# Two weight sums of a row formed before the next row's, operand steps taken two a row up to the fifth warm-up row, and operand sums held behind output weights

## The chip, the cores and the metric

The kernel runs on one core of one Trainium2 chip. The metric is the device time of one execution in microseconds (us). Three runs of the kernel before gave 2141.2, 2142.65 and 2145.68 us; the median is 2142.65 us. A run of this kernel can tell a difference of about 0.2% (4.3 us) from no change.

## The reference, cut to what matters

One Conformer-style layer over 1152 token columns (1024 of a prompt and 8 x 16 of running streams), all in fp32: a SwiGLU half step, a mixer (a gated delta rule beside pooling), a second SwiGLU half step, a final norm.

```python
def swiglu(x, w_gate, w_up, w_down):
    return (jax.nn.silu(x @ w_gate) * (x @ w_up)) @ w_down
...
x = x + 0.5 * swiglu(rms_norm(x, norm_ffn1[l]), w_ffn1_gate[l], w_ffn1_up[l], w_ffn1_down[l])
m, s_new, conv_new, pool_new = mixer(rms_norm(x, norm_mix[l]), ...)
x = x + m
x = x + 0.5 * swiglu(rms_norm(x, norm_ffn2[l]), w_ffn2_gate[l], w_ffn2_up[l], w_ffn2_down[l])
```

The width is 1024 and the hidden width of SwiGLU is 2816, which is 22 rows of 128. All three edits of the change lie in the two half steps; the mixer between them is not touched.

## The kernel before, in words

**Operands in two parts.** TensorE multiplies fp32r values. Each fp32 weight or activation is therefore split in two: ScalarE casts it to a high part (`hi`, line 288 or 186), and VectorE subtracts that from the original to get the low part (`lo`, line 289 or 187). A product is three matmuls: high by high, high by low, low by high (line 59).

**Columns.** The 1152 columns are three chunks: chunk 0 has 512, chunks 1 and 2 have 320 each. Chunks 1 and 2 form the two column halves of a Strassen-Winograd 2 x 2 scheme, in which seven products (named B11, B21, B22, T1, T2, T3, T4) do the work of eight. The code calls this pair "1"; chunk 0, cut in two halves of 256, is pair "0".

**`gate_up`, the first part of a half step.** It forms `silu(x @ w_gate) * (x @ w_up)` row by row.

- Warm-up: the first ten rows are computed for chunk 0 directly, two products of 24 matmuls for each of gate and up. Beside them a generator `build` (the function `operands`) prepares the Winograd operands of pair 1 in 15 steps: norms of chunks 1 and 2 (sums of squares, a 128x1 matmul with `ones`, `rt` on VectorE at line 232, a power on GpSimd at line 233, a matmul with `ident` that spreads it), scaling (line 337), seven combinations (lines 300 to 317) with their splits (line 328). After its end the same calls take up to eight scaling steps (line 372) of `build0`, which prepares the same for pair 0. Lines 605 to 606 call `built()` two or three times a row.
- Row phase: then every row is done in Winograd form, for pair 1 alone (rows 8, 9, 0 to 3), for both pairs (10 to 21), and for pair 1 alone again (4 to 7). In the six rows before the first one with both pairs the remaining 22 steps of `build0` run as well, at four places of a row.

**One row in the row phase (class `Row`).** A row has four weight blocks of 128x512 floats: `w[0]`, `w[1]` from the gate matrix, `w[2]`, `w[3]` from the up matrix. Three blocks go to TensorE as they are (B11, B21, T4) and four as sums, formed by GpSimd:

- sum 1 = `w[2] + w[3]`, for T1 (line 283),
- sum 2 = sum 1 + `w[0]`, for T2 (line 287; one buffer, `sum`),
- sum 4 = sum 2 + `w[1]`, for B22 (line 283),
- sum 3 = `w[0] + w[2]`, for T3 (line 283).

Sums 1, 3 and 4 take the two buffers of the ring `s` (in the region Q) in turn, in the order in which the code asks for them. A sum's buffer is free again when ScalarE and VectorE have split the sum that stood in it. TensorE's order in a steady row is T1 of the next row, T3 of this one, then B11 and B21 of the next, T4 of this one, T2 and B22 of the next. The split operands rotate through seven buffers O0 to O6, so the splits of a row run up to seven products ahead of the matmuls; in the steady rows O0 holds T2, O1 holds B22, O2 holds T1, O3 holds T3, O4 B11, O5 B21 and O6 T4.

**Reading the products.** Four of the products pile up in one PSUM tile: B11, then T2, T3 and T4 are added onto it. Between them VectorE must have read the tile: line 498 (`c2 = al - c3`) after T2 and before T3, line 512 (`c3 = c3 - al`) after T3 and before T4, line 523 after T4. These instructions stand in VectorE's queue among the splits (line 289), the operand steps of `build0` (lines 351, 358, 367) and, for finished groups of two rows, the sums of the generator `combine` (lines 300 to 317, 414, 415). An engine executes its queue in order.

**`downs`, the second part of a half step.** `down0` multiplies chunk 0 by the output weights, whose units are split by `split_unit` (lines 186, 187). Beside it a generator `sums()` takes four groups of raw rows that `gate_up` has put into DRAM (regions x10, x11, x20, x21 after loading, line 846) through `combine` and splits each result (lines 858, 859) into the regions B0 to B6, for `down12` to use later. `tc.issue_after(ins)` is an order for the scheduler: of the instructions in its block, those on the engine of `ins` are put behind `ins`.

Of the kernel before, what the change touches and what calls it, by code (L numbers as in the profile page):

```python
# [7 lines left out]
F32 = mybir.dt.float32  # L8
# [32 lines left out]
def trunk(ctx: ExitStack, tc: tile.TileContext, xin, s0, convst, poolst, cm_in, vec_in, small_in,  # L41
# [3 lines left out]
    V, A, G, T, SY = nc.vector, nc.scalar, nc.gpsimd, nc.tensor, nc.sync  # L45

    class Products:

        t = 0.0
# [98 lines left out]
    W = {}  # L148
# [33 lines left out]
    def split_unit(unit, e=None):  # L182
        i, raw = unit
        m = raw.shape[-1]
        hi, lo = [region(t, F32R)[:, :m] for t in W["splits"][i % len(W["splits"])]]
        A.copy(hi, raw)  # L186
        (e or V).tensor_sub(lo, raw, hi.bitcast(F32))  # L187
        return [t.rearrange("p (k c) -> p k c", c=P) for t in (hi, lo)]

    def load_mix(src, kind):  # L190
# [78 lines left out]
    class Blocks:  # L269


        def __init__(self, ring):
            self.gs, self.ring, self.n, self.e = Slots(), ring, 0, G

        def piece(self, *src, more=None):

            m = src[0].shape[-1]
            t = region(self.ring[self.n % len(self.ring)], F32R)
            self.n += 1
            hi, lo = t[:, :m], t[:, 512:512 + m]  # L280
            if len(src) == 2:
                t = self.gs.get("s", m)
                self.e.tensor_add(t, *src)  # L283
                src = [t]
            src = src[0]
            if more:
                G.tensor_add(more[0], src, more[1])
            Blocks.high = A.copy(hi, src).ins  # L288
            Blocks.mark = V.tensor_sub(lo, src, hi.bitcast(F32)).ins  # L289
            return [x.rearrange("p (k c) -> p k c", c=P) for x in (hi, lo)]  # L290
# [95 lines left out]
    def gate_up(wi, wg, wu, gk, H, RB, cs, ahead, norm, x0=None):  # L386


        bl = Blocks([f"O{(i + 6) % 7}" for i in range(7)])
        gs, piece, product = bl.gs, bl.piece, bl.product  # L390
# [62 lines left out]
        class Row:  # L453
# [19 lines left out]
            def left_gate(self):  # L473

                self.al, self.p1, self.row = {}, {}, {}
                w = piece(self.w[0])
                for c in self.pairs:
                    self.al[c] = self.into("da"[c], c, w, "B11")
                    if c:
                        self.p1[c] = gs.get("p1", N)  # L480
                    else:
                        self.row = cs.get("row", N0)
                        self.p1[c] = self.row[:, :N0 // 2]
                    A.copy(self.p1[c], self.al[c])
                w = piece(self.w[1])
                for c in self.pairs:
                    ga, p1 = self.into("b", c, w, "B21"), self.p1[c]
                    V.tensor_add(p1, p1, ga)
                    A.activation(p1, p1, AF.Silu)

            def right_gate(self):

                self.c2 = {}
                w = piece(self.sm)
                for c in self.pairs:
                    self.c2[c] = gs.get("c2", N) if c else self.row[:, N0 // 2:]
                    product(self.al[c], w, (op0, op)[c]["T2"], False)
                    V.tensor_sub(self.c2[c], self.al[c], self.c3[c])  # L498
                step()
                w = piece(self.sm, self.w[1])  # L500
                for c in self.pairs:
                    de, c2 = self.into("b", c, w, "B22"), self.c2[c]
                    V.tensor_add(c2, c2, de)
                    A.activation(c2, c2, AF.Silu)

            def right_up(self):

                w = piece(self.w[0], self.w[2])
                for c in self.pairs:
                    c2, c3 = self.c2[c], self.c3[c]  # L510
                    product(self.al[c], w, (op0, op)[c]["T3"], False)
                    V.tensor_sub(c3, c3, self.al[c])
                    V.tensor_mul(c2, c2, c3)
                    if c:
                        gated(self.f, 2, c2)
# [77 lines left out]
        for f in range(2 if x0 else 0, ahead):  # L593
            g1, g2, u1, u2 = load(f)
            pg, pu = pt("b")[:, :N0], pt("a")[:, :N0]
            done = gated0(f, pg, pu)
            product(pg, piece(g1), H0[0], True, False)
            product(pg, piece(g2), H0[1], False, True)
            next(done)
            product(pu, piece(u1), H0[0], True, False)  # L600
            built()
            product(pu, piece(u2), H0[1], False, True)
            next(done)
            built()
            if f > 1:
                built()
        for _ in build:
            pass
# [230 lines left out]
    def downs(wd, gk, src, done0=None, after0=lambda: (), done12=None, ends=lambda: None):  # L839
# [12 lines left out]
        def sums():  # L852
            for _ in range(4):
                yield
            for q in range(RAW // 2):
                def put(name, src):
                    hi, lo = [op0[name][s][q] for s in range(2)]
                    A.copy(hi, src)
                    V.tensor_sub(lo, src, hi.bitcast(F32))  # L859

                yield from combine(*stage[q], put)

# [700 lines left out]
    for n in names:  # L1563
        if n[1] in "dHXr":
            continue
        b, w, h = n[0], n[1], n[2]
# [40 lines left out]
    while left or fill or live or cur:  # L1607
# [8 lines left out]
        if cand and (not cand[0][0] or cur is None or cur[1] > cand[0][1]):  # L1616
            n = cand[0][-1]
            e = live[n]
# [204 lines left out]
```

## Time and profile before

| what | value |
|---|---|
| median of three runs | 2142.65 us (2141.2 to 2145.68) |
| the profiled execution | 2141.4 us |
| its span, first to last instruction | 2139.6 us |
| TensorE (PE) busy | 98% of the span |
| VectorE (DVE) busy | 71% |
| ScalarE (ACT) busy | 45% |
| GpSimd (POOL) busy | 23% |
| granted TensorE clock, mean | 0.998 |

The profile calls the engines PE (matmul), PEld (weight load), DVE, ACT, POOL and SP (the queue of the transfers). In a list of waits a row names the engine, the tile that the waiting instruction writes, its line, the engine and line waited for, then the total in us, the count and the longest. In a timeline a row gives the start, the length, the engine, line, operation and tiles, the count of merged instructions and, in brackets, the idle time before and what ended it. In a table of windows each row gives the length of the window and then PE, PEld, DVE, ACT and POOL busy in it.

### The profile page before, as it was taken

Reading aid. Unit: us, or ns where it says so; the run is one execution under the profiler, and the core shown is the slowest. Engines: PE = TensorE matmul, PEld = TensorE weight load, DVE = VectorE, ACT = ScalarE, POOL = GpSimd, SP = SyncE. Lnnn points to the kernel's source line nnn. Section 1 sums busy time; section 2 is a strip of 40 time slices with the busy share of each in tenths; the row PEclk is TensorE's granted clock in tenths of the full one; section 3 lists DMA queues with packets and bytes.
Section 4 is the critical chain, followed back from the end, with each engine's and each line's share of the span. In section 5 each row is a group of like instructions: output and inputs, shape, how many; then the busy total and the mean of one; then the engine's idle time right before and its main releaser. Section 6 shows DMA issues by size and latency. Waiting matters only on the chain.

```text
span 2139.6 us, 34979 instructions
## 1 busy us (share of the span) xinstructions
PE 2100.1 (98%) x13219; PEld 1941.3 (91%) x13219; DVE 1509.4 (71%) x2948; ACT 955.9 (45%) x1974; POOL 496.7 (23%) x471
## 2 busy tenths in 40 slices
PE   9999999999999999999999999999999999999997
PEld 7799999999789998888999998889999999988997
DVE  7989555567537887878687877888955556744887
ACT  6445344444313445645555545544534444422333
POOL 1244343332001200100111100224534333200121
PEclk9999999999999999999999999999999999999999
DMA  7333333357465732112222122443333335746572
GB/s 258 131 114 125 110 119 110 133 197 259 123 239 175 278 99 72 50 61 64 69 91 82 54 92 92 167 138 108 125 110 119 110 134 190 263 131 243 187 275 80
DMA packets 106136, 298.21 MB, mean 139 GB/s; under 512 B 16624, under 2 KB 24688, under 8 KB 105712
## 3 DMA queue, kind: packets, MB, share of 16 engines
q1 hardware_dynamic: 104672, 294.63, 40.1%
q8 instruction: 104, 1.70, 0.3%
q10 hardware_dynamic: 1296, 1.36, 0.2%
q14 instruction: 64, 0.52, 0.1%
HBM read 223.28 MB, written 72.66 MB: 138 GB/s over the span
## 4 chain that ended last, share of the span: by engine, by line
PE 83%; DVE 10%; issue 3%; ACT 2%; POOL 1%; DMA 1%; POOLq 0%; DVEq 0%; SPq 0%; ACTq 0%
PE ps_a L59 32%; PE ps_d L59 21%; PE ps_b L59 19%; PE ps_c L59 10%; DVE O L289 3%; DVE O L187 1%; PE ps_b L63 1%; ACT O L186 0%; DVE A L367 0%; DVE B L1090 0%; DVE A L1229 0%; DVE A L1230 0%; DMA g_keep<-x 0%; ACT O L288 0%; DVE B L859 0%
## 5 line engine op out<-in xcount | busy, mean ns | idle before, releaser
L59 PE MATMUL ps_a<-B,O 128*128 128x320 f32 x3040 | 505.5, 310 | 7.8 <-DVE x L498 5.8
L59 PEld LDWEIGHTS ps_a<-B,O 128*128 128x128 f32 x3040 | 457.1, 188 | 13.2 <-DVE x L498 7.5
L59 PE MATMUL ps_a<-A,O 128*128 128x320 f32 (+1 forms) x2048 | 447.4, 355 | 2.0 <-DVE x L739 1.8
L59 PEld LDWEIGHTS ps_a<-A,O 128*128 128x128 f32 x2048 | 347.1, 189 | 40.1 <-ACT O L288 2.3
L59 PE MATMUL ps_d<-A,O 128*128 128x512 f32 (+1 forms) x1632 | 321.1, 353 | 2.6 <-ACT O L186 1.6
L59 PEld LDWEIGHTS ps_d<-A,O 128*128 128x128 f32 x1632 | 270.5, 189 | 49.0 <-ACT O L186 3.9
L289 DVE TENSOR_TENSOR O<-Q,O 128x512 fp32r<-128x512 f32 (+1 forms) x238 | 197.2, 831 | 109.8 <-ACT O L288 108.9
L288 ACT CAST O<-Q 128x512 fp32r<-128x512 f32 (+1 forms) x238 | 142.8, 604 | 175.6 <-POOL Q L283 43.5
L59 PE MATMUL ps_b<-A,O 128*128 128x256 f32 (+2 forms) x1128 | 208.1, 334 | 5.4 <-ACT O L288 5.3
L289 DVE TENSOR_TENSOR O<-R,O 128x512 fp32r<-128x512 f32 (+1 forms) x204 | 159.9, 789 | 59.0 <-ACT O L288 58.4
L59 PE MATMUL ps_b<-B,O 128*128 128x320 f32 x1248 | 200.8, 309 | 0.0
L59 PEld LDWEIGHTS ps_b<-A,O 128*128 128x128 f32 x1128 | 175.2, 191 | 26.2 <-ACT O L288 5.7
L59 PEld LDWEIGHTS ps_b<-B,O 128*128 128x128 f32 x1248 | 186.4, 188 | 0.0
L288 ACT CAST O<-R 128x512 fp32r<-128x512 f32 (+1 forms) x204 | 123.8, 612 | 105.5 <-PE ps_d L59 34.4
L186 ACT CAST O<-R 128x1024 fp32r<-128x1024 f32 (+1 forms) x86 | 85.8, 1009 | 165.9 <-PE ps_d L59 121.7
L59 PE MATMUL ps_c<-B,O 128*128 128x320 f32 x912 | 144.9, 309 | 0.6 <-DVE O L289 0.6
L59 PEld LDWEIGHTS ps_c<-B,O 128*128 128x128 f32 x912 | 136.0, 188 | 1.3 <-DVE O L289 0.9
L187 DVE TENSOR_TENSOR O<-R,O 128x1024 fp32r<-128x1024 f32 (+1 forms) x86 | 101.8, 1190 | 49.2 <-ACT O L186 29.4
L444 POOL TENSOR_TENSOR A<-A,A 128x512 fp32r<-128x512 f32 x44 | 71.0, 1613 | 248.6 <-ACT A L443 248.4
L59 PE MATMUL ps_d<-B,O 128*128 128x320 f32 (+1 forms) x576 | 117.4, 348 | 0.8 <-DVE x L1111 0.7
L59 PEld LDWEIGHTS ps_d<-B,O 128*128 128x128 f32 x576 | 92.7, 190 | 9.6 <-DVE x L1111 2.1
L414 ACT CAST x<-x 128x320 fp32r<-128x320 f32 x98 | 44.8, 458 | 96.6 <-DVE x L523 32.8
(334 smaller groups left out, 3012.5 us busy)
## 6 DMA issues: line engine op xcount, KB each, us to landing
g_keep<-x SPq DMA_DIRECT2D x98, 320.0 KB, 2.6
R<-in_wu SPq DMA_DIRECT2D x51, 512.0 KB, 3.8
R<-in_wg SPq DMA_DIRECT2D x50, 512.0 KB, 3.8
R<-in_wd SPq DMA_DIRECT2D x48, 512.0 KB, 3.8
g_keep<-A SPq DMA_DIRECT2D x44, 512.0 KB, 3.8
A<-g_keep SPq DMA_DIRECT2D x44, 512.0 KB, 6.0
B<-g_keep SPq DMA_DIRECT2D x56, 320.0 KB, 6.6
A<-g_keep SPq DMA_DIRECT2D x42, 320.0 KB, 4.9
```

What stands on the lines that cost most here:

```text
L59: self.put(nc.tensor.matmul(out, lhs, rhs, **k), n / 2400 + .003 if lhs.dtype == F32R else max(n, lhs.shape[-1]) / 600)
L63: self.put(nc.tensor.transpose(out, lhs, rhs), out.shape[-1] / 1200)
L186: A.copy(hi, raw)
L187: (e or V).tensor_sub(lo, raw, hi.bitcast(F32))
L288: Blocks.high = A.copy(hi, src).ins
L289: Blocks.mark = V.tensor_sub(lo, src, hi.bitcast(F32)).ins
L414: A.copy(go[:, 0], src)
L444: G.tensor_sub(go[:, 1], row, go[:, 0].bitcast(F32))
```

## The change

It has three parts.

1. A method `total` forms a sum of two blocks without splitting it. Sum 4 is now asked for in `left_gate`, right after the split of `w[1]`, and sum 3 in `right_gate`, right after the split of sum 4 and so before the next row's sum 1 and sum 2. The order in which the ring `s` is used becomes sum 4, sum 3, next sum 1, where it was sum 4, next sum 1, sum 3.
2. In the warm-up, the third call of `built()` in a row starts with row 5 instead of row 2 (`f > 4` for `f > 1`). In the first half step the calls of the warm-up are then 22 instead of 25, and one of the eight scaling steps of `build0` moves into the row phase; in the second half step they are 25 instead of 28, and all eight stay.
3. `split_unit` notes its VectorE instruction in `W["mark"]`, and the splits of `sums()` in `down0` are traced under `tc.issue_after(W["mark"])`.

```diff
@@ split_unit
-        (e or V).tensor_sub(lo, raw, hi.bitcast(F32))
+        W["mark"] = (e or V).tensor_sub(lo, raw, hi.bitcast(F32)).ins
@@ class Blocks
+        def total(self, a, b):
+
+            t = self.gs.get("s", a.shape[-1])
+            self.e.tensor_add(t, a, b)
+            return t
+
         def piece(self, *src, more=None):
...
-            if len(src) == 2:
-                t = self.gs.get("s", m)
-                self.e.tensor_add(t, *src)
-                src = [t]
-            src = src[0]
+            src = self.total(*src) if len(src) == 2 else src[0]
@@ Row.left_gate
                 w = piece(self.w[1])
+                self.s4 = bl.total(self.sm, self.w[1])
@@ Row.right_gate
                 step()
-                w = piece(self.sm, self.w[1])
+                w = piece(self.s4)
+                self.s3 = bl.total(self.w[0], self.w[2])
@@ Row.right_up
-                w = piece(self.w[0], self.w[2])
+                w = piece(self.s3)
@@ gate_up, warm-up
             built()
-            if f > 1:
+            if f > 4:
                 built()
@@ downs, sums()
                     hi, lo = [op0[name][s][q] for s in range(2)]
-                    A.copy(hi, src)
-                    V.tensor_sub(lo, src, hi.bitcast(F32))
+                    with tc.issue_after(W["mark"]):
+                        A.copy(hi, src)
+                        V.tensor_sub(lo, src, hi.bitcast(F32))
```

**GpSimd in the row phase.** Before, at row 0 (the third of the row phase). Q is the region of the ring `s`, x21 holds sum 2, R0 to R3 are raw weights.

```order
L287 TENSOR_TENSOR x21_131_996<-Q_46_117,R3_50_121 128x512
L283 TENSOR_TENSOR Q_46_117<-R1_48_119,R2_49_120 128x512
L283 TENSOR_TENSOR Q_46_117<-x21_131_996,R3_50_121 128x512
L283 TENSOR_TENSOR Q_46_117<-R1_48_119 128x512
L287 TENSOR_TENSOR x21_131_996<-Q_46_117,R0_47_118 128x512
```

These are sum 2 of row 0, sum 3 of the row ahead of it, sum 4 of row 0, sums 1 and 2 of the next row. Now, in the same row:

```order
L278 TENSOR_TENSOR Q_46_117<-Q_46_117 128x512
L289 TENSOR_TENSOR x21_131_995<-Q_46_117,R3_50_121 128x512
L278 TENSOR_TENSOR Q_46_117<-R3_50_121,Q_46_117 128x512
L278 TENSOR_TENSOR Q_46_117<-x21_131_995,R3_50_121 128x512
L417 TENSOR_TENSOR x20_130_994<-x10_128_992,x20_130_994 128x320
L278 TENSOR_TENSOR Q_46_117<-R1_48_119 128x512
```

These are sums 1, 2, 3 and 4 of row 0 one after the other (line 278 is the sum, line 289 sum 2), then an operand sum and sum 1 of the next row. A row's four sums now stand together, and sum 1 takes the buffer of the sum 4 ahead of it, where it took that of a sum 3.

**VectorE in the same row.** Its queue has the same kinds of instructions in the same order; only the operand step between two splits is a neighbouring one. Now:

```order
L291 TENSOR_TENSOR O1_151_1202<-Q_46_117,O1_151_1202 128x512
L369 TENSOR_TENSOR A0_153_1221<-x00_33_104,A0_153_1221 128x512
L291 TENSOR_TENSOR O2_154_1226<-Q_46_117,O2_154_1226 128x512
L516 TENSOR_TENSOR x21_131_995<-x21_131_995,ps_a_135_1020 128x320
L517 TENSOR_TENSOR x11_129_993<-x11_129_993,x21_131_995 128x320
L291 TENSOR_TENSOR O3_156_1245<-Q_46_117,O3_156_1245 128x512
```

Before, the same six stood as O1 at line 289, line 367, O2, lines 512 and 513, O3. Between the split of sum 4 (O1) and that of sum 1 (O2) there is one operand step, before and now.

**TensorE in the warm-up.** Before, the 128x1 matmuls of the second norm and the matmuls that spread its result (first half step):

```order
L59 MATMUL ps_d_82_514<-ones_67,B6_66_321 128x1 x3
L59 MATMUL ps_b_85_532<-A0_35_106,O1_87_534 128x512
L59 MATMUL ps_b_85_532<-A2_37_108,O1_87_534 128x512
L59 MATMUL ps_b_85_532<-A0_35_106,O1_87_534 128x512 x2
L59 MATMUL ps_b_85_532<-A2_37_108,O1_87_534 128x512
L59 MATMUL ps_b_85_532<-A0_35_106,O1_87_534 128x512 x2
L59 MATMUL ps_b_85_532<-A2_37_108,O1_87_534 128x512
L59 MATMUL ps_b_85_532<-A0_35_106,O1_87_534 128x512
L59 MATMUL ps_d_84_521<-ident_66,rt_83_518 128x128 x3
```

Now:

```order
L59 MATMUL ps_d_87_565<-ones_67,B6_66_321 128x1 x3
L59 MATMUL ps_a_83_517<-A1_36_107,O4_89_572 128x512
L59 MATMUL ps_a_83_517<-A3_38_109,O4_89_572 128x512
L59 MATMUL ps_a_83_517<-A1_36_107,O4_89_572 128x512 x2
L59 MATMUL ps_a_83_517<-A3_38_109,O4_89_572 128x512
L59 MATMUL ps_a_83_517<-A1_36_107,O4_89_572 128x512 x2
L59 MATMUL ps_a_83_517<-A3_38_109,O4_89_572 128x512
L59 MATMUL ps_a_83_517<-A1_36_107,O4_89_572 128x512 x2
L59 MATMUL ps_a_83_517<-A3_38_109,O4_89_572 128x512
L59 MATMUL ps_a_83_517<-A1_36_107,O4_89_572 128x512
L59 MATMUL ps_d_90_592<-ident_66,rt_88_569 128x128 x3
```

The `ones` group stands 36 matmuls later than before and the `ident` group 39 later; 12 weight matmuls lie between them where 9 did. In the second half step 31 row matmuls are added ahead of the spreading ones.

**ScalarE at the start of `down0`.** Before, ahead of the fourth unit of output weights (O4 from R0), the casts of raw rows from x11 and x10:

```order
L858 CAST B4_449_5236<-x11_442_5226 128x320
L858 CAST B0_445_5232<-x11_442_5226 128x320
L858 CAST B1_446_5233<-x10_441_5224 128x320
L858 CAST B2_447_5234<-x10_441_5224 128x320
L858 CAST B4_449_5236<-x10_441_5224 128x320
L186 CAST O4_463_5310<-R0_454_5243 128x768
```

Now:

```order
L863 CAST B2_447_5234<-x11_442_5226 128x320
L863 CAST B4_449_5236<-x11_442_5226 128x320
L863 CAST B1_446_5233<-x10_441_5224 128x320
L863 CAST B2_447_5234<-x10_441_5224 128x320
L863 CAST B4_449_5236<-x10_441_5224 128x320
L186 CAST O4_463_5310<-R0_454_5243 128x768
```

The three casts from x10 still stand ahead of that unit on ScalarE. On VectorE, whose instruction is the mark, the 28 splits of a half step and the combinations between them are now spread over the units up to the end of `down0`'s first part; before, all but one of them stood ahead of the eighth unit.

## The prediction

> **What bounds the kernel now.** The page comes first: span and busy time by engine.
>
> ```profile
> span 2139.6 us, 34979 instructions
> PE 2100.1 (98%) x13219; PEld 1941.3 (91%) x13219; DVE 1509.4 (71%) x2948; ACT 955.9 (45%) x1974; POOL 496.7 (23%) x471
> ```
>
> PE is the bound. The change neither adds nor removes a matmul, so it can only change how long PE waits, 39.5 us of the span by this line, or runs stretched behind a late operand. The list of PE's waits (total, count, longest) shows which of them the edits can touch.
>
> ```profile
> PE ps_a L59 <- DVE x L498: 5.8, 5, 1.8
> PE ps_b L59 <- ACT O L288: 5.3, 1, 5.3
> PE ps_d L59 <- POOL rt L233: 3.4, 4, 2.4
> PE ps_d L59 <- ACT O L186: 1.6, 3, 1.2
> PE ps_a L59 <- DVE x L512: 1.1, 2, 0.6
> ```
>
> L498 and L512, VectorE's readings of the piled-up products, belong to the row phase (edit 1); rt L233 to the warm-up (edit 2); O L186 to `down0` (edit 3). The 5.3 us of O L288 is one wait. None of the edits moves the kernel's opening, so I leave it. Next the table of windows: the length, then PE, PEld, DVE, ACT and POOL busy, then the granted clock. The first two windows are the six rows for pair 1 alone ahead of the rows with both pairs, in each half step; the third lies in the rows for pair 1 alone at the end; the other four are single steady rows from L498 to L498.
>
> ```profile
> 126.36:205.05 78.69, 75.21 (x506) 73.60 (x505) 78.27 (x103) 41.69 (x84) 39.36 (x28) 1.00 0.38 126
> 1462.85:1540.51 77.66, 73.74 (x493) 72.13 (x492) 76.54 (x103) 41.13 (x83) 39.58 (x28) 1.00 0.37 123
> 470.00:520.00 50.00, 50.00 (x347) 50.00 (x347) 39.44 (x60) 25.33 (x49) 19.45 (x15) 1.00 0.74 261
> 134.70:147.50 12.80, 12.80 (x90) 12.80 (x89) 12.77 (x18) 6.21 (x13) 5.85 (x4) 1.00 0.26 84
> 147.50:163.20 15.70, 14.67 (x97) 13.95 (x96) 15.66 (x23) 7.10 (x15) 8.26 (x6) 1.00 0.38 131
> 163.20:177.80 14.60, 12.82 (x84) 12.32 (x84) 14.57 (x20) 8.94 (x18) 8.56 (x6) 1.00 0.51 179
> 177.80:190.59 12.79, 12.26 (x83) 12.20 (x84) 12.76 (x19) 5.77 (x12) 5.87 (x4) 1.00 0.34 109
> ```
>
> A row of pair 1 has seven products of twelve weight loads, 84, and PEld is busy 12.32 us with them when it is fed. In the six rows DVE is busy 99% (78.27 of 78.69), and PE loses 78.69 − 73.60 = 5.09 us there, in the second half step 77.66 − 72.13 = 5.53, together 10.62. So here DVE sets the pace: the single rows last 12.8 to 15.7 us with DVE full. In the closing rows PE fills its 50.00 us and DVE 39.44: an edit that costs DVE something is paid for in the six rows and hidden there.
>
> **Edit 1: the order of the sums.** Here is DVE's timeline in the first of those single rows (start, length, line, tiles), then POOL's, and one cast of ACT.
>
> ```profile
> 136.10 1.66 DVE L289 TENSOR_TENSOR O<-Q,O 128x512 fp32r<-128x512 f32 x1
> 137.68 0.68 DVE L367 TENSOR_TENSOR A<-x,A 128x512 fp32r<-128x512 f32 x1
> 138.28 1.78 DVE L289 TENSOR_TENSOR O<-Q,O 128x512 fp32r<-128x512 f32 x1
> 139.99 0.47 DVE L512 TENSOR_TENSOR x<-x,ps_a 128x320 f32<-128x320 f32 x1
> 140.50 1.37 DVE L513 TENSOR_TENSOR x<-x,x 128x320 f32<-128x320 f32 x1
> 143.99 1.38 DVE L289 TENSOR_TENSOR O<-R,O 128x512 fp32r<-128x512 f32 x1
> ```
>
> ```profile
> 135.91 1.30 POOL L287 TENSOR_TENSOR x<-Q,R 128x512 f32<-128x512 f32 x1 [4.49 <-issue]
> 137.84 1.68 POOL L283 TENSOR_TENSOR Q<-R,R 128x512 f32<-128x512 f32 x1 [0.63 <-DVE O L289]
> 140.21 1.31 POOL L283 TENSOR_TENSOR Q<-x,R 128x512 f32<-128x512 f32 x1 [0.69 <-DVE O L289]
> 143.25 1.57 POOL L283 TENSOR_TENSOR Q<-R 128x512 f32<-128x512 f32 x1 [1.74 <-DMA R<-in_wu]
> ```
>
> ```profile
> 139.55 0.62 ACT L288 CAST O<-Q 128x512 fp32r<-128x512 f32 x1 [1.49 <-POOL Q L283]
> ```
>
> A DVE instruction of this size with two inputs in SBUF takes 0.68 us free and 1.37 to 1.78 while a POOL sum runs; L512, with one input in PSUM, takes 0.47. L513, half as large, I put at 0.47 free. So the four sums cost DVE 1.66 − 0.68 = 0.98 (sum 2), 1.78 − 0.68 = 1.10 (sum 3), 1.37 − 0.47 = 0.90 (sum 4) and 1.38 − 0.68 = 0.70 (sum 1): 3.68 us a row.
>
> Now with the new order of the ring's two buffers. Sum 1 takes the buffer of the previous sum 4, so it waits until O1 (B22) has been split; before, it waited for a split done long ago, and its result lay ready when DVE came to O2. In DVE's queue O1 and O2 are one operand step apart. From the end of O1: the operand step, 0.60 start to start (137.68 to 138.28); sum 1, 1.30 (the length of 135.91); the cast, 0.62, beside which POOL runs sum 2 at once, 1.30, and blocks the split; the split itself, 0.60. That is 0.60 + 1.30 + 1.30 + 0.60 = 3.80 us from the end of O1 to that of O2. Before it was 2.30 (137.76 to 140.06), and without sums 1.20. Queued behind the waiting split are L512 and all later splits of the row; PE's T3 waits for L498, and T4 for L512. Sums 1 and 2 then cost 2.60, sum 3, now let go by O2, costs L513's 0.90 in sum 4's place, and sum 4, let go by O3, the 1.10 of a split: 4.60. That is 0.92 us a row more than 3.68.
>
> Where DVE is full this is PE's time. Of the six rows, four have the four sums alone: 4 × 0.92 = 3.7. The other two (147.50 and 163.20, POOL x6) have operand sums of `combine` as well, which already spread the sums apart; I take 0.4 for both together. That is 4.1 a half step, **+8.2** in both. Bounds: 0 where the sums cost what they did, and 1.5 (3.80 − 2.30, with nothing saved on sums 3 and 4) in five rows of two half steps, 15.0. I take 8.2, nearer to the middle, because it is the walk along the quoted rows. A gain is the first rival. Where DVE has slack (the closing rows, 39.44 of 50.00) the step costs nothing: PE's operands lie up to seven products ahead. Sums 3 and 4 need no block that the sums 1 and 2 or a split of the row hadn't needed by then, so none of SP's loads is waited for sooner; a load that starts sooner finds the transfer engines 0.26 to 0.51 busy in these rows.
>
> One statement of the Trainium skill speaks on this price: "Perfetto Trace Analysis", section "GPSIMD Engine Instruction", calls recorded spans of that engine unreliable in part. If a sum holds DVE only for the mean 0.92 that DVE loses (3.68 / 4) instead of 1.30, sums 1 and 2 cost 1.84 against 0.98 + 0.70 = 1.68; with sums 3 and 4 at 2.00 the row is 3.84, 0.16 more, and the same rows give 1.4 in place of 8.2.
>
> **Edit 2: the warm-up.** PE's timeline around the second norm of the first half step, the two instructions between, and the same place in the second half step:
>
> ```profile
> 57.07 0.72 PE L59 MATMUL ps_d<-ones,B 128*128 128x1 f32 x6
> 57.65 2.31 PE L59 MATMUL ps_b<-A,O 128*128 128x512 f32 x9
> 62.31 0.93 PE L59 MATMUL ps_d<-ident,rt 128*128 128x128 f32 x6 [2.35 <-POOL rt L233]
> 60.76 0.14 DVE L232 TENSOR_SCALAR rt<-ps_d 128x3 f32<-128x3 f32 x1
> 60.97 1.29 POOL L233 TENSOR_TENSOR rt<-rt,vec 128x3 f32<-128x3 f32 x1 [10.03 <-DVE rt L232]
> 1387.04 0.94 PE L59 MATMUL ps_d<-ident,rt 128*128 128x128 f32 x6 [0.39 <-POOL rt L233]
> ```
>
> DVE's L232 runs at 60.76, 3 us after the `ones` group, because it is queued behind earlier steps; then POOL takes 1.29. Only nine matmuls (2.31 us) cover this. Now twelve do (2.31 × 12 / 9 = 3.08), a row's spacing later when DVE has had fewer steps to run; L232, 0.14, and POOL, 1.29, then fit into 3.08 with 1.65 to spare. So **−2.35** (if DVE were again 3 us late, 3.08 − 3.0 − 1.43 leaves 1.35 of it). In the second half step 31 matmuls more, about 8 us, stand ahead of the spreading ones: **−0.39**. In the first half step one scaling step moves into the DVE-full rows:
>
> ```profile
> L372 DVE SCALAR_TENSOR_TENSOR x<-x,vec,A x8: 740/743/1784, 85.2 to 106.7; 128x512 f32<-128x512 f32 x8
> ```
>
> Its median is 0.74 us; between 0 and that I take **+0.4**, since the last step only slides to the end of the six rows.
>
> **Edit 3: the held splits.** The timeline at the start of `down0`:
>
> ```profile
> 529.99 4.64 DMA x<-g_keep
> 534.62 1.17 ACT B L858 x3
> 535.79 1.68 ACT O L186 x2
> 536.58 1.20 PE L59 MATMUL ps_d<-A,O 128*128 128x512 f32 x4 [1.21 <-ACT O L186]
> ```
>
> The 1.21 us stall comes from ACT: its three casts of raw rows wait for a transfer that ends at 534.62, and the unit's cast L186 stands behind them. The mark is an instruction of DVE, so only DVE's halves of the splits are held; in ACT's order the three casts stand ahead of L186 as before. So the stall stays: **0**, between −0.4 (less DVE work between the units) and +0.6 (a split of the next units later). In the second half step this stage loses a few tenths at most. The held DVE work must be done before `down12` and has the rest of `down0` as cover.
>
> **The sum.** The profiled execution took 2141.4 us, 1.8 more than its span. 2141.4 + 8.2 + 0.4 − 2.35 − 0.39 + 0 = 2147.3. The median of the runs shown is 2142.65, 1.25 above: **2148.5 us**.
>
> **The rivals.**
>
> *Faster: forming the sums ahead takes POOL's chain off ACT and DVE.* The page's group of casts waits for those sums most:
>
> ```profile
> L288 ACT CAST O<-Q 128x512 fp32r<-128x512 f32 (+1 forms) x238 | 142.8, 604 | 175.6 <-POOL Q L283 43.5
> ```
>
> If the early sums 3 and 4 let DVE run ahead, PE's 10.62 us shrink; all of it with edit 2 gives 2142.65 − 2.74 − 10.62 = 2129.3, half 2134.6. Against it: PE's waits name DVE's L498 and L512, not POOL or ACT O in this stage, and DVE is 99% busy, so ready operands don't help it. It decides if DVE's loss a row falls from 3.68 below 3.68 − (12.80 − 12.32) = 3.2, where the shortest of these rows comes down to PE's 12.32. Chance 0.2.
>
> *The same: each sum costs DVE what it did.* The blocked time only changes its place; edit 2 remains: 2142.65 − 2.74 = 2139.9. For it: four sums a row, before and after. Against it: before, each sum cost 0.70 to 1.10 of its 1.3, partly hidden beside L512 and idle moments, and the new chain leaves none for sums 1 and 2. Chance 0.32. The Trainium skill, "SBUF — State Buffer", section "Who interferes with whom", says that a DVE instruction with two SBUF inputs and a GpSimd one that reads SBUF exclude each other for a whole instruction, and one with a single SBUF input isn't touched. By that rule each sum costs up to its whole length wherever it stands, which is this rival; the trace agrees on which are blocked (1.37 to 1.78 against L512's 0.47).
>
> *Slower* is the forecast, 0.48. Its mechanism shows from (4.3 + 2.74 − 0.4 − 0.8) / 8 = 0.73 us more a row on: below that, the gain of edit 2 and the 4.3 us that can be told from no change cover it.
>
> **How the numbers follow.** The forecast's own range is the sum with 0 to 15.0 for edit 1: 2140.3 to 2155.3. The whole range reaches down to half of the faster rival, about 2135, and up to 2155. About 0.2% (4.3 us) is what a measurement can tell from no change; that band is 2138.4 to 2146.9. Faster needs the first rival at nearly half strength: 0.2. The same takes the second rival's 0.32 and 0.03 of the forecast, where its price is small: 0.35. Slower: the other 0.45.
>
> **What would show it.** In the changed profile: six-row windows longer by some 4 us each with PEld unchanged; 3.8 us between the ends of O1's and O2's splits; O2's cast waiting for POOL and sum 1 for DVE's O1; PE's wait at the second norm gone; the stall after `down0`'s x10 transfer still there. I am wrong if the windows keep their length or shrink, if O1 to O2 stays at 2.3 us, or if a stall outside these places changes by more than 1 us.

## The result and the profile after

The changed kernel took 2148.75 us (median of 8 runs, 2146.5 to 2152.71) against 2142.76 us before (8 runs, 2140.19 to 2145.68): a ratio of 1.0033, 95% interval 1.0024 to 1.0043. It is slower, by 6 us. The forecast was 2148.5. Two single executions among the later runs, 2556 us with the third buffer (at a granted clock of 0.75) and 11786 us with sum 4 alone ahead, are left out of the ratios below; without them the medians given there would be less than 0.2 us lower.

The page of the changed kernel, and its list of PE's waits (L516 was L512 before, L501 was L498, L290 and L291 were L288 and L289):

```profile
span 2147.2 us, 34945 instructions
PE 2102.7 (98%) x13219; PEld 1945.2 (91%) x13219; DVE 1510.1 (70%) x2948; ACT 954.7 (44%) x1974; POOL 500.6 (23%) x471
```

```profile
PE ps_a L59 <- DVE x L516: 9.4, 10, 1.9
PE ps_b L59 <- ACT O L290: 6.0, 1, 6.0
PE ps_a L59 <- DVE x L501: 4.9, 7, 1.2
...
PE ps_d L59 <- ACT O L186: 2.0, 2, 1.3
...
PE ps_d L59 <- POOL rt L233: 0.6, 2, 0.5
```

PE waits for VectorE's two readings of a row 14.3 us instead of 6.9 (5.8 + 1.1), and for the norm's rt 0.6 instead of 3.4. So most of the loss is where the prediction put it, and the gain too. The six rows ahead of the rows with both pairs, in each half step (length, PE, PEld, DVE, ACT, POOL, granted clock), from the first product of pair 1 to the first of pair 0:

```profile
121.19:203.71 82.52, 75.68 (x494) 73.69 (x492) 72.98 (x105) 41.22 (x83) 39.48 (x27) 0.98 0.35 113
1463.92:1545.19 81.27, 75.44 (x493) 73.70 (x492) 70.22 (x103) 41.66 (x83) 39.16 (x27) 0.98 0.36 116
```

The same window before, in the first half step (the second is the row of 77.66 in the prediction):

```profile
126.36:203.61 77.25, 73.77 (x494) 72.16 (x492) 76.86 (x103) 41.03 (x83) 38.50 (x28) 1.00 0.37 123
```

They are 5.27 and 3.61 us longer now. DVE was full there; now it idles for 9.5 and 11 us of them. Its timeline, and then GpSimd's (POOL), shows what it waits for in the first steady row, that is from one L501 to the next:

```profile
131.75 0.68 DVE L291 TENSOR_TENSOR O<-Q,O 128x512 fp32r<-128x512 f32 x1
132.35 0.68 DVE L369 TENSOR_TENSOR A<-x,A 128x512 fp32r<-128x512 f32 x1
134.88 1.24 DVE L291 TENSOR_TENSOR O<-Q,O 128x512 fp32r<-128x512 f32 x1 [1.85 <-ACT O L290]
136.04 0.47 DVE L516 TENSOR_TENSOR x<-x,ps_a 128x320 f32<-128x320 f32 x1
136.54 1.36 DVE L517 TENSOR_TENSOR x<-x,x 128x320 f32<-128x320 f32 x1
...
139.03 1.78 DVE L291 TENSOR_TENSOR O<-R,O 128x512 fp32r<-128x512 f32 x1
```

```profile
132.50 1.69 POOL L278 TENSOR_TENSOR Q<-Q 128x512 f32<-128x512 f32 x1 [5.43 <-DVE O L291]
134.27 1.30 POOL L289 TENSOR_TENSOR x<-Q,R 128x512 f32<-128x512 f32 x1
136.25 1.30 POOL L278 TENSOR_TENSOR Q<-R,Q 128x512 f32<-128x512 f32 x1 [0.69 <-DVE O L291]
138.59 1.68 POOL L278 TENSOR_TENSOR Q<-x,R 128x512 f32<-128x512 f32 x1 [1.03 <-DVE O L291]
```

Sum 1 starts only when O1 has been split, after 5.43 us of idle GpSimd; O2's split waits for its cast; L516 is queued behind. In this row PE does not wait yet. In the next one, GpSimd has an operand sum (L417) ahead of sum 1, VectorE idles longer, and PE waits:

```profile
146.40 1.77 POOL L417 TENSOR_TENSOR x<-x,x 128x320 fp32r<-128x320 f32 x1 [6.13 <-ACT x L416]
148.13 1.29 POOL L278 TENSOR_TENSOR Q<-R 128x512 f32<-128x512 f32 x1
150.11 1.22 DVE L291 TENSOR_TENSOR O<-Q,O 128x512 fp32r<-128x512 f32 x1 [2.68 <-ACT O L290]
151.87 5.29 PE L59 MATMUL ps_a<-B,O 128*128 128x320 f32 x24 [1.85 <-DVE x L516]
```

In the first steady row, from the end of O1's split (132.43) to that of O2's (136.12) it is 3.69 us; 3.80 was forecast, and it was 2.30 before. The rows from one L501 to the next last 13.59, 16.79, 15.25 and 13.56 us, and lasted 12.80, 15.70, 14.60 and 12.79.

### The profile page after: what moved, and what is told of

It is laid out like the page before. It is cut to its first block, busy times and chain, and to the rows that moved or that the text cites. A ratio compares the mean times of both kernels' runs of the same rounds, so it can differ in the third digit from the quotient of the medians.

```text
span 2147.2 us, 34945 instructions
## 1 busy us (share of the span) xinstructions
PE 2102.7 (98%) x13219; PEld 1945.2 (91%) x13219; DVE 1510.1 (70%) x2948; ACT 954.7 (44%) x1974; POOL 500.6 (23%) x471
## 4 chain that ended last, share of the span: by engine, by line
PE 80%; DVE 7%; issue 4%; POOL 3%; DMA 2%; ACT 2%; SPq 0%; POOLq 0%; ACTq 0%; DVEq 0%
PE ps_a L59 31%; PE ps_d L59 21%; PE ps_b L59 18%; PE ps_c L59 10%; POOL Q L278 2%; DVE O L291 2%; DVE O L187 1%; DMA g_keep<-x 1%; PE ps_b L63 1%; ACT O L290 1%; ACT O L186 1%; DMA A<-g_keep 1%; DVE B L1095 0%; POOL A L446 0%; DVE A L1234 0%
## 5 line engine op out<-in xcount | busy, mean ns | idle before, releaser
L291 DVE TENSOR_TENSOR O<-Q,O 128x512 fp32r<-128x512 f32 (+1 forms) x238 | 191.1, 804 | 138.2 <-ACT O L290 137.3
L290 ACT CAST O<-Q 128x512 fp32r<-128x512 f32 (+1 forms) x238 | 141.7, 605 | 166.7 <-POOL Q L278 42.5
L291 DVE TENSOR_TENSOR O<-R,O 128x512 fp32r<-128x512 f32 (+1 forms) x204 | 155.1, 765 | 51.9 <-ACT O L290 51.4
L290 ACT CAST O<-R 128x512 fp32r<-128x512 f32 (+1 forms) x204 | 123.6, 612 | 95.5 <-PE ps_d L59 33.8
L186 ACT CAST O<-R 128x1024 fp32r<-128x1024 f32 (+1 forms) x86 | 85.8, 1008 | 135.4 <-PE ps_d L59 80.1
L278 POOL TENSOR_TENSOR Q<-R 128x512 f32<-128x512 f32 (+1 forms) x40 | 55.0, 1374 | 174.1 <-DVE O L291 132.3
```

Of the source, the lines that this page charges most:

```text
L278: self.e.tensor_add(t, a, b)
```

## The experiments

Each run is set against runs of the kernel before on the same chip; ratios are with their 95% intervals. "The six rows" are the windows of above, 77.25 and 77.66 us before, of which TensorE's weight loads need 72.15.

**Each edit alone.** Edit 1 (edits 2 and 3 taken back):

```diff
-            if f > 4:
+            if f > 1:
-                    with tc.issue_after(W["mark"]):
-                        A.copy(hi, src)
-                        V.tensor_sub(lo, src, hi.bitcast(F32))
+                    A.copy(hi, src)
+                    V.tensor_sub(lo, src, hi.bitcast(F32))
```

> Edit 1 alone (sums 3 and 4 ahead), the warm-up and the output stage as before. Theory (sum 1 takes the ring buffer of the sum 4 ahead of it and so waits for VectorE's split of it): the whole loss is here, about 4 us in each of the two stretches of six rows and about 1 us in each of the two closing stretches, together +8 to +10 us; the end of O1's split to the end of O2's is about 3.7 us. Rival (the held splits or late transfers in the output stage make the loss): +3 us or less. Second rival (each sum costs VectorE what it did): 0.

Measured: 2154.55 us, ratio 1.0066 (1.0053 to 1.0080). The six rows:

```profile
125.47:206.74 81.27, 74.15 (x493) 72.15 (x492) 70.20 (x103) 41.66 (x83) 39.22 (x27) 1.00 0.36 116
1467.84:1549.11 81.27, 74.15 (x493) 72.15 (x492) 70.21 (x103) 41.67 (x83) 39.18 (x27) 1.00 0.35 115
```

They are 4.02 and 3.61 us longer, as forecast, and the rows for pair 1 alone at the end ("the closing stretches") are 1.05 and 1.17 longer up to the last row. The whole loss of the change is here; by the ratio it is 14 us, more than expected, while the two profiled executions differ by 10.6 (a span of 2150.2 against 2139.6). At least 1.6 us of that is a loss which the changed kernel does not show, at the first reading (L501) of the last row of each half step:

```profile
521.98 0.46 ACT L862 CAST B<-x 128x320 fp32r<-128x320 f32 x1 [3.34 <-DMA x<-g_keep]
522.47 0.49 DVE L863 TENSOR_TENSOR B<-x,B 128x320 fp32r<-128x320 f32 x1 [1.75 <-ACT B L862]
524.70 0.48 DVE L501 TENSOR_TENSOR x<-ps_a,x 128x320 f32<-128x320 f32 x1
525.24 2.03 PE L59 MATMUL ps_a<-B,O 128*128 128x320 f32 x12 [0.97 <-DVE x L501]
```

An operand split of `down0` (L863) waits for a late transfer, stands in VectorE's queue ahead of the reading, and PE waits 0.97 us (0.67 in the second half step). With edit 3, in the changed kernel, no such split stands ahead of that reading, and PE has no such wait. No run has edits 1 and 3 without edit 2, so that edit 3 is the reason is likely but not shown.

Edit 2, put into the kernel before:

```diff
-            if f > 1:
+            if f > 4:
```

> Edit 2 alone (third operand step from row 5 on). Theory: PE's wait of 2.35 us at the second norm of the first half step and that of 0.39 in the second are gone, one scaling step moves into the full rows: -2.3 us, between -2.7 and -1.8. Rival (the waits only move, since VectorE's work in the warm-up is the same): 0, with a wait of over 1 us for the rt of another norm or at the start of the row phase.

Measured: 2139.52 us, ratio 0.9992 (0.9981 to 1.0002): 1.7 us less by the ratio, and not told apart from none. In the trace the warm-ups lose 2.62 and 0.64 us, as forecast or better, but the first six rows last 1.51 us longer (78.76); the second do not (77.64).

Edit 3, put into the kernel before:

```diff
+                    with tc.issue_after(W["mark"]):
-                    A.copy(hi, src)
-                    V.tensor_sub(lo, src, hi.bitcast(F32))
+                        A.copy(hi, src)
+                        V.tensor_sub(lo, src, hi.bitcast(F32))
```

> Edit 3 alone (splits held behind the output weights' splits on VectorE). Theory: ScalarE's three casts of the late transfer still stand ahead of the unit's cast, so the wait for O L186 stays at 0.5 to 1.3 us in the first half step: 0 in all, between -0.5 and +1. Rival (the held work lengthens the output stage, as the changed kernel's second half step with 1.3 us for O L186 in place of 0.2 suggests): +1 to +2.5 us.

Measured: 2140.51 us, ratio 0.9996 (0.9986 to 1.0005): no difference. The waits for O L186 are 2.4 us here. They are 2.0 in the changed kernel and 1.6 before, and with edit 2 alone, which does not touch this stage, 3.1:

```profile
PE ps_d L59 <- ACT O L186: 3.1, 4, 1.8
```

So this wait differs from execution to execution by as much as edit 3 could do to it.

**Is it the ring's wait, or that the sums stand closer together?** First a third buffer, so that no sum waits for a split of its own row:

```diff
-    SIZE |= {"Q": 2048}
+    SIZE |= {"Q": 2560}
-        gs.place(region("Q"), ("raw", 1024, 1), ("s", 512, 2))
+        gs.place(region("Q"), ("raw", 1024, 1), ("s", 512, 3))
```

> The changed kernel with a third buffer in the ring of the sums, so that no sum has to wait for a split of the same row; order of the sums and all else as changed. Theory (the ring's wait makes the loss): the end of O1's split to the end of O2's falls from 3.7 us to 2.3 or less, VectorE's idle time ahead of O2 goes, and the time falls by 6 to 10 us against the changed kernel, to 2138 to 2143. Rival (four sums close together block VectorE's two-input instructions longer, whatever lets them start): still 2146 to 2151, with instructions of 1.3 to 1.8 us in VectorE's queue where there is idle time now.

Measured: 2142.09 us, ratio 1.0005 (0.9996 to 1.0014). VectorE's timeline in the same row:

```profile
131.32 1.66 DVE L291 TENSOR_TENSOR O<-Q,O 128x512 fp32r<-128x512 f32 x1
132.91 0.68 DVE L369 TENSOR_TENSOR A<-x,A 128x512 fp32r<-128x512 f32 x1
133.51 1.79 DVE L291 TENSOR_TENSOR O<-Q,O 128x512 fp32r<-128x512 f32 x1
135.22 0.47 DVE L516 TENSOR_TENSOR x<-x,ps_a 128x320 f32<-128x320 f32 x1
135.73 1.30 DVE L517 TENSOR_TENSOR x<-x,x 128x320 f32<-128x320 f32 x1
...
138.16 1.78 DVE L291 TENSOR_TENSOR O<-R,O 128x512 fp32r<-128x512 f32 x1
```

O1's end to O2's is 2.32 us (132.98 to 135.30), with no idle time between. The rows are 13.14, 15.94, 14.83 and 13.13 us: of the 0.8 us a row, 0.45 came from the ring and about 0.3 is left. That rest is the rival's part, a longer hold: as before, four instructions of VectorE are held up in a row, but they take 1.66, 1.79, 1.30 and 1.78 us where they took 1.66, 1.78, 1.37 and 1.38, which is 0.34 more. The wait in the closing stretch is gone.

Then sum 4 alone ahead, sum 3 at its old place:

```diff
-                self.s3 = bl.total(self.w[0], self.w[2])
-                w = piece(self.s3)
+                w = piece(self.w[0], self.w[2])
```

> The changed kernel with sum 3 formed at its old place and only sum 4 ahead, so that the ring is used in the order of before (sum 4, next sum 1, sum 3) and sum 1 no longer stands behind the split of the same row's sum 4. Theory (the ring's order): the row phases lose the 4 us each that edit 1 alone costs, the wait of 0.8 us in each closing stretch goes, and the time is 2138 to 2142, below before by what edit 2 brings. Rival (sums that stand closer together make the loss, whichever they are): halfway, 2143 to 2147.

Measured: 2138.99 us, ratio 0.9980 (0.9971 to 0.9989). The steady rows are 12.81, 15.99, 14.58 and 12.81 us, those of edit 2 alone (12.80, 16.02, 14.60, 12.81), and no wait is left in the closing stretches. So sum 4's place costs nothing, and sum 3's all of it.

**Where edit 2's gain goes.** One call more in the last warm-up row, so that all scaling steps stay in the warm-up:

```diff
-            if f > 1:
+            if f > 4:
+                built()
+            if x0 and f == ahead - 1:
                 built()
```

> Edit 2 alone, with one more call in the last warm-up row of the first half step, so that all eight scaling steps stay in the warm-up. In the profile of edit 2 alone the first six rows lost 1.5 us. Theory (that is the scaling step which edit 2 pushes into the rows where VectorE is full): those rows take what they took before, the waits of the warm-up stay gone, and the time is about 3.2 us below before, 2137 to 2140. Rival (the 1.5 us are chance of one execution): as edit 2 alone, no change in the six rows.

Measured: 2141.71 us, ratio 0.9993 (0.9983 to 1.0003). The first six rows are 78.49 us, still 1.24 longer, without the scaling step. It is at most a small part of the 1.51. Then the same steps sooner:

```diff
-            built()
-            if f > 1:
-                built()
+            for _ in range({5: 2, 6: 4, 7: 3}.get(f, 1)):
+                built()
```

> Edit 2's two calls a row up to row 4, then 3, 5, 4, 2 and 2 calls in rows 5 to 9, so that all scaling steps stay in the warm-up and fewer of them lie right ahead of the row phase. With edit 2 alone VectorE is busy 9.84 of the last 11 us ahead of 121 us, where it was busy 5.76 before, and the first six rows lose 1.2 to 1.5 us more. Theory (VectorE enters the row phase with a queue, and its first reading of a row comes 0.6 to 0.9 us later against PE): the six rows of the first half step lose at most 0.5 us more than before, the warm-up's waits stay gone, and the time is 2137 to 2140. Rival (the same work of VectorE in a warm-up that is 2.6 us shorter ends late, wherever its steps stand): still 1.2 us or more, as edit 2 alone.

Measured: 2140.49 us, ratio 0.9992 (0.9982 to 1.0002). The first six rows are 78.00 us, 0.75 longer, between the two expectations. VectorE's load in the last 11 us ahead of the six rows is not lower (9.68 us, where it is 9.37 with edit 2 alone and 6.36 before), so the edit did not relieve that place as meant. Here are before and this run:

```profile
115.36:126.36 11.00, 11.00 (x50) 9.10 (x49) 6.36 (x9) 4.78 (x8) 5.00 (x4) 1.00 0.20 70
```

```profile
111.98:122.98 11.00, 11.00 (x50) 9.09 (x49) 9.68 (x11) 5.59 (x10) 5.57 (x4) 1.00 0.30 101
```

**Is it VectorE's work that sets the pace of the six rows?** Edit 2, with four more operand steps in the last warm-up rows, so that 18 are left for the six rows:

```diff
-            if f > 1:
+            if f > 4:
                 built()
+            for _ in range(((0, 2, 3) if x0 else (0, 1, 1))[max(f - ahead + 3, 0)]):
+                built()
-        scaled = [0] * KT
+        scaled = [0] * (KT + 4)
```

> Edit 2 alone, and four more operand steps (the split of B11 and the difference after it) taken in the last warm-up rows of each half step, so that 18 instead of 22 or 23 are left for the six rows where VectorE is full. Sums and ring as before. Theory (VectorE's work sets the pace of those rows): 4 steps of 0.68 to 1.2 us less in them, of the 5 us that PE loses in each stretch 3 to 4 go; with edit 2's 3.2 the time is 2131 to 2136. Rival (the ring's waits or the transfers of weights set the pace): the six rows keep their length, 2137 to 2140.

Measured: 2142.04 us, ratio 0.9991 (0.9982 to 1.0000). The six rows are 79.77 and 77.85 us: no gain. VectorE's rows in the first half step tell why: 12.80, 15.70, 14.59, then 11.25 and 10.77. The steps are taken in turn, four a row, so those that are missing are missing in the last rows; the two long rows, in which the operand sums run, keep all they had. The 2.2 us that VectorE saves come to nothing at both ends. After its last first reading (L498) the stretch lasts 3.32 us where it lasted 1.65, since TensorE needs 12.32 us for the matmuls of a row whatever VectorE does. And the steps taken sooner make VectorE late: its first reading comes 11.34 us after the start, and 9.07 in the second half step, where it came after 8.34 and 8.35. So the run says that these steps were in the wrong place; it does not test less work in the long rows.

**The price of one sum,** by a fifth one in five rows of each half step of the kernel before, which nothing reads:

```diff
                 w = piece(self.w[0], self.w[2])
+                if "row" not in cs.mem:
+                    G.tensor_add(gs.get("waste", 512), self.w[0], self.w[2])
```

(The ring "waste" has one buffer of 512 in the enlarged region Q.)

> The kernel before, with a fifth sum on GpSimd in each of the rows ahead of those with both pairs, written to a buffer of its own that nothing reads (so no instruction waits for it; it only shares GpSimd and its access to memory with VectorE). It measures the price of one sum. Theory (0.7 to 1.1 us of blocked VectorE for each): a row takes 0.7 to 1.1 us more, five rows in each half step, 2150 to 2154. Rival one (a whole sum's length, 1.3 us and more): 2156 to 2160. Rival two (nearly free): 2143 to 2145.

Measured: 2147.87 us, ratio 1.0032 (1.0019 to 1.0044), 6.9 us over the runs beside it. The sums run ahead of the matmuls, so two of the five (at 99.7 and 109.1 us) still fall into the warm-up. The other three (127.5, 145.4 and 160.3 us) cost 1.11, 1.12 and 1.09 us: the first reading comes 9.45 us after the start where it came after 8.34, and the steady rows are 13.92, 16.79, 14.83 and 12.79 us. The last two of these have no fifth sum and pay 0.23 and nothing. In the second half step the three cost 1.10, 1.13 and 0.70. So a sum costs about what the prediction took for it (0.70 to 1.10), and the total is below the expected one because three of five fall into the stretch. The second of them, and the instruction that it holds up:

```profile
145.42 1.75 POOL L510 TENSOR_TENSOR Q<-R,R 128x512 f32<-128x512 f32 x1
145.93 1.79 DVE L367 TENSOR_TENSOR A<-x,A 128x512 fp32r<-128x512 f32 x1
```

VectorE's instruction ends 0.55 us after GpSimd's (147.72 and 147.17). The same holds for the full-size instructions held up in the prediction's rows: they end 0.54 or 0.55 us after the sum beside them, about the 0.60 that one takes from start to start when free. So VectorE stands still until the sum has ended, and a sum costs what is left of it when VectorE comes to an instruction with two inputs in SBUF.

**The sums on VectorE.** The four sums of the six rows formed there, in the changed kernel:

```diff
-            self.gs, self.ring, self.n, self.e = Slots(), ring, 0, G
+            self.gs, self.ring, self.n, self.e, self.m = Slots(), ring, 0, G, G
-                G.tensor_add(more[0], src, more[1])
+                self.m.tensor_add(more[0], src, more[1])
+        bl.e = bl.m = V
         last, row = None, Row(*order[0], 1)
...
+                bl.e = bl.m = G
                 cs.mem["row"] = cs.mem["sg"] + cs.mem["su"]
```

> The changed kernel with the four sums of a row formed on VectorE instead of GpSimd in the six rows ahead of those with both pairs (on GpSimd again from the first row with both pairs on). Theory (a sum on GpSimd costs VectorE 0.7 to 1.1 us of blocked time and the ring's wait as much again): four sums of 0.6 us on VectorE itself cost 2.4 to 2.7 a row in place of 4.6, with no wait for another engine ahead of sum 1; the row phases fall by 5 us or more each against the changed kernel, to 2136 to 2141. Rival (a sum on GpSimd is nearly free for VectorE): VectorE's full queue gets 2.4 us a row more, five rows in each half step, 2160 and more.

Measured: 2129.40 us, ratio 0.9943 (0.9930 to 0.9955), below the expected range. VectorE in the first steady row, with sums 1 and 2 at lines 278 and 289:

```profile
130.95 0.69 DVE L369 TENSOR_TENSOR A<-x,A 128x512 fp32r<-128x512 f32 x1
131.55 0.69 DVE L278 TENSOR_TENSOR Q<-Q 128x512 f32<-128x512 f32 x1
132.27 0.69 DVE L289 TENSOR_TENSOR x<-Q,R 128x512 f32<-128x512 f32 x1
132.98 0.69 DVE L291 TENSOR_TENSOR O<-Q,O 128x512 fp32r<-128x512 f32 x1
133.59 0.48 DVE L516 TENSOR_TENSOR x<-x,ps_a 128x320 f32<-128x320 f32 x1
133.99 0.68 DVE L291 TENSOR_TENSOR O<-Q,O 128x512 fp32r<-128x512 f32 x1
134.59 0.48 DVE L517 TENSOR_TENSOR x<-x,x 128x320 f32<-128x320 f32 x1
```

In this row no instruction takes 1.4 or 1.8 us any more; a sum costs VectorE 0.6 to 0.7 itself, and VectorE's longest wait for another engine in the row is 0.22 us. The same with sum 3 at its old place (the two diffs of above together):

> The changed kernel with sum 3 at its old place (as in the run with sum 4 alone ahead) and the sums of the six rows on VectorE. Theory: with sums on VectorE the six rows take what they took with all four sums moved, and the wait of about 1 us in each closing stretch, which comes from sum 3's place in the ring, is gone: about 2 us below that run's 2129.4, 2126 to 2129. Rival (sum 3 ahead is what made the sums on VectorE fast, since it stands well ahead of its split): 2133 to 2138.

Measured: 2130.11 us, ratio 0.9946 (0.9933 to 0.9960). The closing waits are gone (1.06 and 1.12 us in the run above), and yet the median is no lower; the 2 us are not seen. Last, the sums on VectorE in the order of before, with edit 2 and without edit 3:

> Edit 2 alone, with the sums of the six rows on VectorE, in the order of before and without edit 3. Theory (the gain comes from taking GpSimd's sums out of VectorE's way, not from their order): 2127 to 2131, six rows at 12.0 to 12.4 us each but for those with operand sums. Rival (the order matters on VectorE as well: a sum stands right ahead of its cast and split, so VectorE waits 0.6 us for the cast of sums 3 and 4): about 1.2 us a row more, 2133 to 2139.

Measured: 2129.40 us, ratio 0.9942 (0.9929 to 0.9954). The six rows:

```profile
123.56:196.18 72.62, 72.39 (x493) 72.15 (x492) 71.12 (x120) 42.18 (x83) 15.75 (x11) 1.00 0.39 132
1455.49:1528.47 72.98, 72.38 (x493) 72.15 (x492) 71.56 (x119) 41.15 (x83) 16.35 (x11) 1.00 0.39 127
```

PE is nearly full: its weight loads need 72.15 of the 72.62 and 72.98 us. The order makes no difference here that can be told, and this version beats the kernel before and the changed one.

## Why the prediction was right, point by point

**Edit 1 in the six rows: right in size and cause.** Forecast 4.1 us a half step; edit 1 alone costs 4.02 and 3.61. The interval from O1 to O2 is 3.69 us for 3.80: sum 1 starts beside the operand step and not behind it, but takes 1.69 for 1.30, so the two come to 1.76 where 1.90 was added up. Sums 3 and 4 cost what was forecast (0.89 and 1.10 for 0.90 and 1.10). In all the row has 1.85 us of idle time and 2.55 of held-up instructions, 4.40 for the forecast's 4.60, and pays 0.79 for 0.92. So the loss is a wait: the time in which sums hold VectorE up fell from 3.68 us a row to 2.55, and its busy time in the six rows from 76.86 to 72.98. The third buffer took 0.45 of the 0.8 us a row away, which shows the ring's wait.

The step that was off is the two rows with operand sums: 0.2 each was taken, on the ground that these already spread the sums apart, and they pay 1.09 and 0.65. In the first of them the operand sum stands ahead of sum 1 and makes the wait longer (2.68 us for 1.85). On the other side only two rows of four sums pay the 0.8, not four: the last one pays nothing in edit 1 alone, and the two ends of the stretch together 0.65. That the sum came out is luck.

**Edit 1 in the closing rows: wrong.** It was put at nothing, since VectorE has slack there and the operands lie up to seven products ahead. The changed kernel loses about 1 us in each, and the trace shows the same chain:

```profile
486.25 0.95 DVE L291 TENSOR_TENSOR O<-Q,O 128x512 fp32r<-128x512 f32 x1 [1.40 <-ACT O L290]
489.26 1.24 DVE L291 TENSOR_TENSOR O<-Q,O 128x512 fp32r<-128x512 f32 x1 [2.06 <-ACT O L290]
490.43 0.47 DVE L516 TENSOR_TENSOR x<-x,ps_a 128x320 f32<-128x320 f32 x1
```

```profile
491.05 3.75 PE L59 MATMUL ps_a<-B,O 128*128 128x320 f32 x24 [0.78 <-DVE x L516]
```

VectorE is idle for 2.06 us and PE waits all the same. The slack of an engine covers work, not a chain through three engines that ends in its queue ahead of what PE needs. With sum 3 at its old place or a third buffer the wait is gone.

**Edit 2: the gain right, its price too small.** The waits at the norms went (−2.62 and −0.64, for −2.35 and −0.39). For the six rows 0.4 us was taken, for the scaling step that moves; it is 1.5, and mostly not for that step, since 1.24 stays without it. In the four runs with edit 2, the ring's order of before and no further steps in the warm-up, VectorE's second row takes 16.0 us in the first half step, as it does in the second half step even before (16.08), where it took 15.70, and its first reading comes 0.4 to 0.9 us later against the start of the stretch (8.34 us after it before, 8.76 to 9.25 now, but 8.36 in the second half step of edit 2 alone). So VectorE enters these rows later. What goes with it is VectorE's load just ahead: in the first half step it is busy 9.35 to 9.78 of the last 11 us in these four runs, for 6.36 before; in the second it is 6.4 before and with edit 2 alike, and there the stretch is no longer either (77.64 for 77.66). That fits a queue which VectorE carries over. No run lowered that load, so it is not shown.

**Edit 3: right.** Alone it makes no difference that can be measured, and the stall behind the late transfer is still there. That it may spare PE the wait at the last row's first reading, when edit 1 is in, was not foreseen.

**The rivals.** The faster one, that sums formed ahead free the six rows, did not happen; its size was reached by another edit, since taking the sums off GpSimd gives about 12 us, edit 2's part included. The rival of no change fell with edit 1 alone, and the third buffer's run adds that even without the ring's wait a row pays 0.3 us for the new places. The rule of the Trainium skill ("SBUF — State Buffer", section "Who interferes with whom"), by which the two exclude each other for a whole instruction, agrees with the traces: a held-up instruction ends 0.54 or 0.55 us after the sum. The price of a sum is then up to its length, and here it was less, 1.12 us where GpSimd's record shows 1.75, since VectorE came to its instruction 0.51 us after the sum had begun. The rule makes the price depend on where a sum stands (the last instruction held up in a row takes 1.78 us with the third buffer, 1.38 before), so it does not mean that nothing changes. The price of 1.4 us for edit 1, with a sum that holds VectorE for 0.92 us only, is not borne out: the cast of sum 1 starts at 134.22 us, when the whole record of sum 1 has ended (134.19).

**The sum.** Of the terms, by the single edits' traces: 7.6 us for the six rows, 2.2 for the closing rows, −3.3 for the warm-ups, 1.5 for VectorE's later start: 8.1, where 5.85 was forecast and 6.0 measured (5.1 to 9.2 by the interval). The closing rows and the later start were missing in the forecast. The profiles also differ where no edit explains it. From the first matmul to those at 46.06 us before and 43.49 us after, whose order no edit changes, the changed kernel's execution took 3.2 us less (37.53 for 40.76; the profiles of all the runs lie between 37.5 and 40.8). Behind the last product of pair 1 in the second half step it took 1.9 us more (282.11 for 280.26; without edit 3 the profiles reach 281.39). So part of the agreement with 2148.5 is chance.

## What to carry to other kernels

A ring shared by several producers' results is a set of waits: moving one request ahead changes which buffer every later one gets, and so for whom it waits; look for the consumer that stands one step behind. In a stretch where VectorE is full, count what a GpSimd instruction costs VectorE beside what it saves: here a sum of 0.6 us on VectorE cost it up to 1.1 us from GpSimd, and the better move was the opposite one. Work taken out of a stretch helps only in the rows that are too long: four operand steps taken out of the others gave nothing.

## What was not expected of the hardware

After a wait of 1.85 us in the second steady row of the changed kernel, the granted clock went to half for about 3.4 us. The last three columns of a row are the clock, the busy share of the transfer engines, and GB/s:

```profile
152.00:153.00 1.00, 1.00 (x7) 1.00 (x8) 1.00 (x1) 0.00 (x0) 0.74 (x1) 0.87 0.06 16
153.00:154.00 1.00, 1.00 (x6) 1.00 (x5) 1.00 (x3) 0.83 (x3) 0.23 (x1) 0.50 0.00 0
...
155.00:156.00 1.00, 1.00 (x5) 1.00 (x5) 1.00 (x2) 0.00 (x0) 0.24 (x1) 0.50 0.00 0
```

With edit 1 alone PE waited as long in the same row (1.80 us for L516) at a clock of 1.00, and the next reading was then waited for 1.71 us. The rows took the same 16.8 us in both, so the slower matmuls cost nothing here: VectorE set the pace. The length of the wait does not decide it. In the six-row stretches of all the traces eight waits, of 1.74 to 2.49 us, were followed by a clock of one half, each time for about 3.4 us, and fourteen others, of 1.70 to 1.96 us, were not.
